# An expert-dispatch kernel: first input tile loaded in two pieces, and every third product computed on ScalarE

## The chip, the core and the metric

The kernel runs on one core of one Trainium2 chip. The core has several engines that run side by side, each with its own in-order stream of instructions: VectorE (DVE in the profile), ScalarE (ACT), GpSimd (POOL), SyncE (SP), and TensorE, which this kernel does not use. Data moves between the chip's main memory (HBM) and the on-chip memory (SBUF, 128 partitions) by 16 DMA engines. A DMA is issued by an instruction on one of the engines' streams and then runs on its own; another instruction that needs its data waits for its landing. The metric is device time in microseconds (us) of one execution, lower is better.

## The reference

The name speaks of dispatching tokens to experts, but the expert indices are not used in the result: each token's row is written twice, each time multiplied by one of that token's two weights.

```python
batch, seq, hidden, n_experts = 16, 1024, 512, 8
k = 2
"x":              (batch, seq, hidden) float32
"expert_weights": (batch, seq, k)      float32

x_expanded = x[:, :, np.newaxis, :].repeat(k, axis=2)
weights = expert_weights[..., np.newaxis]
return (x_expanded * weights).astype(np.float32)
```

There are 16,384 tokens of 512 float32 values. The input x is 33.5 MB and the output, with two scaled copies of every row, 67.1 MB. There is one multiplication for each output element.

## The kernel before

The 16,384 tokens are dealt to the 128 partitions, 128 consecutive tokens to each (`A_TOTAL` is 128). So a partition owns a contiguous stretch of x and a contiguous stretch of the output, and any group of tokens is a plain slice along the free dimension.

All weights are loaded once into `w_tile` (128 partitions x 256 numbers, 128 KB), by a DMA that SP issues (L45).

The loop on L47 runs over eight input tiles of `TX` = 16 tokens per partition. Each `x_tile` holds 128x8192 float32 numbers, 4 MB, and is loaded by one DMA that ScalarE issues (L49). ScalarE does nothing else in this kernel: its stream is eight load issues in order. `x_pool` has two buffers, so loads 0 and 1 are issued at the start, and load i+2 waits until the products of tile i are done.

Each input tile is worked off in two output tiles of `TO` = 8 tokens (L52). An `o_tile` is 128x8192 float32 as well, since every token has two rows: 4 MB again. It is filled by 16 VectorE instructions (L59), each of which multiplies one token's 512 numbers in every partition by one column of `w_tile`. Then SP issues the store of that output tile (L67). `o_pool` has four buffers, so the first product of output tile n+4 waits until the store of output tile n has landed. There are 16 stores and 256 products in all.

Two queues of DMA work come of this: the loads issued by ScalarE, and the weights and stores issued by SP. Both run on the same 16 DMA engines. The order of instructions on each engine is that of the program text, apart from small moves by the scheduler of the tile framework; the waits are put in by the framework, from the tiles' buffers.

Of the kernel before, what the change touches and what calls it, by code (L numbers as in the profile page):

```python
# [1 line left out]

# [4 lines left out]


@with_exitstack
def kernel(  # L10
    ctx: ExitStack,
    tc: tile.TileContext,
    x: bass.AP,
    expert_indices: bass.AP,
    expert_weights: bass.AP,
    out: bass.AP,
):
    nc = tc.nc

    batch, seq, hidden = x.shape  # L20
    k = expert_weights.shape[-1]
    P = nc.NUM_PARTITIONS
    ntok = batch * seq
    assert ntok % P == 0
    A_TOTAL = ntok // P

    xr = x.rearrange("b s h -> (b s) h").rearrange("(p a) h -> p (a h)", a=A_TOTAL)
    outr = out.rearrange("b s k h -> (b s) (k h)").rearrange(
        "(p a) n -> p (a n)", a=A_TOTAL
    )  # L30
    wr = expert_weights.rearrange("b s k -> (b s) k").rearrange(
        "(p a) k -> p (a k)", a=A_TOTAL
    )
    f32 = mybir.dt.float32
    row = k * hidden

    TX = 16
    TO = 8

    w_pool = ctx.enter_context(tc.tile_pool(name="w_pool", bufs=1))  # L40
    x_pool = ctx.enter_context(tc.tile_pool(name="x_pool", bufs=2))
    o_pool = ctx.enter_context(tc.tile_pool(name="o_pool", bufs=4))

    w_tile = w_pool.tile([P, A_TOTAL * k], f32)
    nc.sync.dma_start(out=w_tile, in_=wr)  # L45

    for i in range(A_TOTAL // TX):  # L47
        x_tile = x_pool.tile([P, TX * hidden], f32)
        nc.scalar.dma_start(  # L49
            out=x_tile, in_=xr[:, i * TX * hidden : (i + 1) * TX * hidden]  # L50
        )
        for j in range(TX // TO):  # L52
            o_tile = o_pool.tile([P, TO * row], f32)
            for t in range(TO):
                at = (j * TO + t) * hidden
                for kk in range(k):
                    c = (i * TX + j * TO + t) * k + kk
                    o = t * row + kk * hidden
                    nc.vector.tensor_scalar(  # L59
                        out=o_tile[:, o : o + hidden],  # L60
                        in0=x_tile[:, at : at + hidden],
                        scalar1=w_tile[:, c : c + 1],
                        scalar2=None,
                        op0=mybir.AluOpType.mult,
                    )
            first = (i * TX + j * TO) * row
            nc.sync.dma_start(out=outr[:, first : first + TO * row], in_=o_tile)  # L67


# [1 line left out]
_INS = ['x', 'expert_indices', 'expert_weights']  # L71
_OUTS = [((16, 1024, 2, 512), 'float32')]


# [23 lines left out]
```

## Time and profile before

| What | Value |
|---|---|
| Median of 6 runs | 242.32 us |
| Lowest and highest run | 241.01 and 243.82 us |
| The profiled execution's own time | 243.82 us |
| Span of the profiled execution, first to last instruction | 242.0 us |
| VectorE busy | 102.4 us, 42% of the span |
| Bytes moved by DMA | 100.81 MB |
| First load and weight load issued | 0.73 us |
| First product starts | 13.56 us |
| First store issued | 20.0 us |
| Last store issued | 209.1 us |

The profiled execution is the slowest of the six runs. Its span leaves out 1.8 us that lie around the first and the last instruction.

The page of the profile gives for each engine its busy time, then a strip of 40 equal slices of the span (about 6 us each), in which a digit is the busy share in tenths; for the DMA engines there is a strip of the same kind and a row of GB/s. A stretch is busy with DMA when its digit is 9. A row of the groups gives the line of the program, the engine, the operation, the tiles, the number of instructions, their busy time, the mean duration of one, and the idle time before them with what ended it. A view by windows gives the same for stretches that one picks: busy time of each engine with the number of instructions, the clock of TensorE, the busy share of the DMA engines, and the rate in GB/s. There, a DMA packet is counted whole, in the stretch where it ends, so that a short stretch can show a share above 1.

The eight loads were issued at 0.73, about 1.2, 26.35, 39.02, 65.40, 99.63, 128.56 and 158.85 us of the span.

### The profile page before, as it was taken

How to read it: one execution, taken by the hardware profiler on the slowest of the kernel's cores; microseconds unless marked ns; L12 is line 12 of the kernel's file. 1: busy time of each engine (PE TensorE's matmuls, PEld its weight loads, DVE VectorE, ACT ScalarE, POOL GpSimd, SP SyncE). 2: the span in 40 equal slices, each digit the busy share in tenths (PEclk: the TensorE clock that was granted, in tenths of full speed). 3: DMA queues.
4: the chain of work that ended last, by engine and by line, in shares of the span. 5: the costliest groups of instructions: out<-in, count | busy, mean ns of one | idle time of the engine just before them, and what ended most of it. 6: DMA issues, size and time to landing. Idle time of an engine off the chain costs nothing.

```text
span 242.0 us, 358 instructions
## 1 busy us (share of the span) xinstructions
DVE 102.4 (42%) x256; POOL 0.2 (0%) x4
## 2 busy tenths in 40 slices
DVE  0079994039803706490082820839008295500000
POOL 0000000000000000000000000000000000000000
DMA  7999999999999999999999999999999999999992
GB/s 276 439 433 422 433 348 428 433 433 417 433 433 428 433 433 433 433 428 433 395 433 433 433 433 433 435 428 433 433 422 433 433 433 433 433 433 433 433 433 97
DMA packets 3602, 100.81 MB, mean 417 GB/s; under 512 B 400, under 2 KB 528, under 8 KB 528
## 3 DMA queue, kind: packets, MB, share of 16 engines
q1 hardware_dynamic: 2448, 67.24, 64.6%
q10 hardware_dynamic: 1152, 33.55, 33.2%
q14 instruction: 2, 0.02, 0.0%
HBM read 33.69 MB, written 67.11 MB: 416 GB/s over the span
## 4 chain that ended last, share of the span: by engine, by line
DMA 52%; DVE 21%; another core or an unknown queue 13%; issue 0%; DVEq 0%
DMA out_dram<-o_tile 36%; DVE o_tile L59 21%; DMA x_tile<-in_x_dram 16%; DVEq L93 0%; DVEq L59 0%
## 5 line engine op out<-in xcount | busy, mean ns | idle before, releaser
L59 DVE TENSOR_SCALAR o_tile<-x_tile,w_tile 128x512 f32<-128x512 f32 x256 | 102.4, 480 | 106.6 <-DMA out_dram<-o_tile 75.4
L82 POOL MEMSET const-bfloat16-1.0<- 128x1 bf16 x1 | 0.1, 102 | 0.0
L82 POOL MEMSET const-uint8-127<- 128x1 uint8 x1 | 0.1, 102 | 0.0
L82 POOL MEMSET const-float32-1.0<- 128x1 f32 x1 | 0.1, 99 | 0.0
L82 POOL MEMSET const-float32-0.0<- 128x1 f32 x1 | 0.1, 98 | 0.2 <-issue 0.2
## 6 DMA issues: line engine op xcount, KB each, us to landing
out_dram<-o_tile SPq DMA_DIRECT2D x16, 4096.0 KB, 43.9
x_tile<-in_x_dram ACTq DMA_DIRECT2D x8, 4096.0 KB, 25.4
w_tile<-in_expert_weights_dram SPq DMA_DIRECT2D x1, 128.0 KB, 9.2
```

What stands on the lines that cost most here:

```text
L59: nc.vector.tensor_scalar(out=o_tile[:, o : o + hidden], in0=x_tile[:, at : at + hidden], scalar1=w_tile[:, c : c + 1], scalar2=None, op0= ...
L82: nc = _bacc.Bacc("TRN2", target_bir_lowering=False, num_devices=1)
```

## The change

The input tiles stand in a list of pieces; the first tile is loaded by two DMAs of 8 tokens (2 MB each), all others by one DMA of 16 tokens as before. Loads 0 and 1 are issued ahead of the loop, and load i+2 at the end of tile i's turn in the program text. Of the 256 products, those with a column number c that leaves 2 on division by 3 are computed by ScalarE (85 of them), the other 171 by VectorE. Buffers, tile sizes and stores stay: 16 stores of 4 MB, two input buffers, four output buffers.

```diff
+    AHEAD = 2
+    tiles = [[8, 8], [16], [16], [16], [16], [16], [16], [16]]
+    starts = [sum(map(sum, tiles[:i])) for i in range(len(tiles))]
...
-        nc.scalar.dma_start(
-            out=x_tile, in_=xr[:, i * TX * hidden : (i + 1) * TX * hidden]
-        )
+    def load(i):
...
+        x_tiles[i] = x_pool.tile([P, TX * hidden], f32, name="x_tile")
+        at = 0
+        for n in tiles[i]:
+            g = starts[i] + at
+            nc.scalar.dma_start(
+                out=x_tiles[i][:, at * hidden : (at + n) * hidden],
+                in_=xr[:, g * hidden : (g + n) * hidden],
+            )
+            at += n
...
+    def scale(out, in_, c):
+        w = w_tile[:, c : c + 1]
+        if c % 3 == 3 - 1:
+            nc.scalar.mul(out=out, in_=in_, mul=w)
+        else:
+            nc.vector.tensor_scalar(
...
+    for i in range(AHEAD):
+        load(i)
+    for i, pieces in enumerate(tiles):
+        x_tile = x_tiles.pop(i)
...
+        for t in range(sum(pieces)):
...
+                scale(
+                    o_tile[:, o : o + hidden],
+                    x_tile[:, t * hidden : (t + 1) * hidden],
+                    (starts[i] + t) * k + kk,
+                )
+            if t + 1 in ends or (t + 1) % TO == 0:
+                nc.sync.dma_start(
...
+        load(i + AHEAD)
```

In the built program, ScalarE's stream is as follows: the two pieces of load 0 and load 1; a load of the table for its activation function, which waits for the weights; 10 products of tile 0 and one of tile 1; load 2; 10 products of tile 1 and one of tile 2; load 3; 10 products of tile 2 and one of tile 3; load 4; 9 products of tile 3; load 5; 11 products of tile 4; load 6; 11 of tile 5; load 7; and the 21 products of tiles 6 and 7. So loads 2, 3 and 4 stand one product later than in the text, behind the first product of the next tile. VectorE takes 10 or 11 products for each output tile, ScalarE 5 or 6. SP's stream is as before, except that a store now waits for both engines.

More of the change, by code (lines that the diff above doesn't have):

```diff
@@ L38 @@
     TO = 8
+    AHEAD = 2
+    tiles = [[8, 8], [16], [16], [16], [16], [16], [16], [16]]
+    starts = [sum(map(sum, tiles[:i])) for i in range(len(tiles))]
+    assert sum(map(sum, tiles)) == A_TOTAL
     w_pool = ctx.enter_context(tc.tile_pool(name="w_pool", bufs=1))
-    x_pool = ctx.enter_context(tc.tile_pool(name="x_pool", bufs=2))
+    x_pool = ctx.enter_context(tc.tile_pool(name="x_pool", bufs=AHEAD))
     o_pool = ctx.enter_context(tc.tile_pool(name="o_pool", bufs=4))
@@ L45 @@
     nc.sync.dma_start(out=w_tile, in_=wr)
-    for i in range(A_TOTAL // TX):
-        x_tile = x_pool.tile([P, TX * hidden], f32)
-        nc.scalar.dma_start(
-            out=x_tile, in_=xr[:, i * TX * hidden : (i + 1) * TX * hidden]
-        )
[L52 to L67, printed above, removed]
+    x_tiles = {}
@@ new lines, in load @@
+    def load(i):
+        if i >= len(tiles):
+            return
+        x_tiles[i] = x_pool.tile([P, TX * hidden], f32, name="x_tile")
[13 more added lines that the diff above has]
+            nc.vector.tensor_scalar(
+                out=out,
+                in0=in_,
+                scalar1=w,
+                scalar2=None,
+                op0=mybir.AluOpType.mult,
+            )
@@ new lines @@
+    for i in range(AHEAD):
+        load(i)
+    for i, pieces in enumerate(tiles):
+        x_tile = x_tiles.pop(i)
+        ends = [sum(pieces[: j + 1]) for j in range(len(pieces))]
+        first = 0
+        for t in range(sum(pieces)):
+            if t % TO == 0:
+                o_tile = o_pool.tile([P, TO * row], f32)
+            for kk in range(k):
+                o = t % TO * row + kk * hidden
+                scale(
+                    o_tile[:, o : o + hidden],
+                    x_tile[:, t * hidden : (t + 1) * hidden],
+                    (starts[i] + t) * k + kk,
+                )
+            if t + 1 in ends or (t + 1) % TO == 0:
+                nc.sync.dma_start(
+                    out=outr[
+                        :, (starts[i] + first) * row : (starts[i] + t + 1) * row
+                    ],
+                    in_=o_tile[:, first % TO * row : (t % TO + 1) * row],
+                )
+                first = t + 1
+        load(i + AHEAD)
```

## The prediction

> **What bounds the kernel now.** I read the strip of DMA work first, because a kernel that only copies and scales can hardly be bound by anything else.
>
> ```profile
> span 242.0 us, 358 instructions
> DVE 102.4 (42%) x256; POOL 0.2 (0%) x4
> ...
> DMA  7999999999999999999999999999999999999992
> GB/s 276 439 433 422 433 348 428 433 433 417 433 433 428 433 433 433 433 428 433 395 433 433 433 433 433 435 428 433 433 422 433 433 433 433 433 433 433 433 433 97
> DMA packets 3602, 100.81 MB, mean 417 GB/s; under 512 B 400, under 2 KB 528, under 8 KB 528
> ```
>
> The DMA engines are full from the second slice to the last but one, nearly always at 433 GB/s; VectorE is busy for 42%. Next I cut windows by what is in flight: loads alone, the worst slice, loads beside stores, stores alone, the end.
>
> ```profile
> 5.00:21.00 16.00, 7.44 (x19) 0.00 (x0) 1.00 1.02 441
> ...
> 30.00:37.00 7.00, 7.00 (x19) 0.00 (x0) 1.00 1.01 348
> ...
> 132.00:150.00 18.00, 6.42 (x16) 0.00 (x0) 1.00 1.01 435
> ...
> 184.00:236.00 52.00, 17.44 (x44) 0.00 (x0) 1.00 1.00 434
> 236.00:238.00 2.00, 0.00 (x0) 0.00 (x0) 1.00 0.57 246
> 238.00:241.00 3.00, 0.00 (x0) 0.00 (x0) 1.00 0.08 33
> ```
>
> Loads alone go at 441 GB/s (434 to 441, as packets fall into windows), loads beside stores at 435, stores alone at 434. So the rate is the same whatever the mixture; one slice, 30 to 37 us, falls to 348 with the engines no less busy. Last, the waits and the chain:
>
> ```profile
> DVE o_tile L59 <- DMA out_dram<-o_tile: 75.4, 9, 12.9
> DVE o_tile L59 <- DMA x_tile<-in_x_dram: 27.2, 2, 13.6
> ...
> 13.56 12.77 DVE o_tile L59 x32
> 26.33 0.02 issue
> 26.35 26.14 DMA x_tile<-in_x_dram
> ```
>
> VectorE waits for stores to give buffers back, so it is the follower. Load 2, issued at 26.35, lands at 52.49 because it shares the engines. The chain names 32 products at 13.56 as a cause of load 2's issue, but while they ran, the strip shows the DMA engines full: that part of the chain costs nothing.
>
> The span as a sum: 100.81 MB at 434 GB/s are 232.3 us. The rest, 9.7 us, is: the first 5 us, which moved 1.23 MB (81 GB/s for 2 us, 357 for 3) where 434 GB/s would move 2.17, so 2.2 us lost; 30 to 37 us, (434-348) x 7 / 434 = 1.4 us; the last 6 us, which moved 0.59 MB of 2.60, so 4.6 us; and 1.5 us in small dips (116 to 120 us, at 401 GB/s, is 0.3 of it). Outside the span lie 243.82 - 242.0 = 1.8 us.
>
> **The change part by part.** No byte is added or removed except what ScalarE's table load may fetch.
>
> *The first tile in two pieces.* Load 0 lands at 13.54 us; its second half, 2.1 MB at 434 GB/s, is 4.8 us, so the first piece lands at about 8.7 us. The products also need the weights, which landed 9.2 us after their issue at 0.73, at 9.9. The first product thus starts between 8.7 and 9.9 instead of 13.56. This moves work ahead by 4 to 5 us on an engine that is no bound: until about 22 us the DMA engines have loads 0 and 1 to move (8.4 MB / 434 = 19.3 us from about 2.5). Saved on the path that sets the end: 0. The additional DMA is one more issue of 0.37 to 0.46 us on ScalarE, behind which only load 1 waits, and load 1 has 8 us until its turn. In the row, loads 0 and 1 were issued as two DMAs too, and 5 to 21 us shows no seam between them: cost 0. The Trainium skill, "DMA: Bandwidth & Descriptors", section "Anatomy of one DMA", gives for GpSimd-issued DMAs a time of 2.0 us plus bytes over 436 GB/s; if the additional DMA paid that fixed cost on the path, the sum would be 2.0 us more, an estimate against which the seamless 441 GB/s stands. "Perfetto Trace Analysis", section "DMA Optimizations", recommends splitting where the DMA engines are generally idle, and here the strip of nines says they are not.
>
> *A third of the products on ScalarE.* VectorE's 32 products took 12.77 us, 0.40 each, so an output tile took 6.4 us and will take 11 x 0.40 = 4.4 on VectorE. The trace has no ScalarE computation. The nearest row is VectorE's own mean, 0.48 for the same 128x512 product; I bound one ScalarE product by 0.40 (VectorE's pace) and 0.96 (twice its mean) and take 0.48. Six then take 2.4 to 5.8, 2.9 as taken, so an output tile is ready after 4.4 (at the worst 5.8) instead of 6.4. What hides this is the backlog of stores. In the phase with stores alone, one store needs 4.19 MB / 434 = 9.7 us, and three others are queued while one buffer is refilled; the refill would have to take longer than three stores, 29 us, to empty the queue. So ScalarE could cost 5 us a product before it decided. Cost and gain: 0. The Trainium skill, "ScalarE: Activation LUTs", section "What ACT_TABLE_LOAD costs", gives 1283 ns for the table load, and 186 ns plus 0.833 ns an element plus 93 for a pointer operand, 0.71 us here: inside the bounds, and the sum would be the same. The table load itself has no row; between 0 and the 6.4 us of a whole output tile it delays the first store only, under the cover of load 1; I take 0.
>
> *The first store earlier.* 8.7 or 9.9 plus 4.4 gives 13 to 14 us (16 if ScalarE is at its bounds) instead of 20.0. From about 15 us the store takes half the engines' time from load 1. What is left of load 1 then, 8.4 - (15 - 2.5) x 0.434 = 3.0 MB, goes at half the rate and lands near 29 us instead of 23. The total in flight is the same.
>
> *Load issues behind products.* Load 2 needs the products of tile 0 on both engines, done near 18 us, but it stands behind the first ScalarE product of tile 1, which needs load 1: it issues near 30 us instead of 26.35. Load 3 waits for load 2's landing, load 4 for load 3's, where before load 3 was issued at 39.02, 13 us before load 2 landed. An issued load needs some time before bytes flow: load 0 took 12.81 us for 9.7 us worth of bytes, so 3.1. So loads 2, 3 and 4 each begin 3 to 4 us after the one before has ended; loads pause more in this stretch than before. Queued on ScalarE behind the waiting product are the load and the rest of that tile's products, all of which need the same landing. The cover is the stores: at 29 us store 0's rest and store 1 (5 MB, 12 us) are queued, at 52 us stores 2 and 3 (8.4 MB, 19 us), at 74 us some three stores. Each exceeds 4 us by far. Price: 0, and 3 x 4 = 12 us if the cover were gone. Loads 5 to 7 wait for the same stores as before.
>
> *The rate while reads and writes mix.* Loads beside stores ran for some 117 us before (30 to 90, 104 to 123, 132 to 151, 163 to 182) and lost 1.4 + 0.3 + about 0.5 = 2.2 us there, 2%. Now 14 us of mixing are added (15 to 29 us). At the mean that is 0.3 us; the bounds are 0 (132 to 150 us lost nothing) and 20% of 14, 2.8 us (30 to 37 us). I take 0.1, since most mixed stretches lost nothing.
>
> Sum on the profiled execution: 243.82 + 0.1 = 243.9. That execution was the slowest of six; the median of the runs lies 1.5 us below it, about what its dip at 30 to 37 us cost. Against the median, 242.32 + 0.1, I predict 242.4 us.
>
> **Rivals.** *A, slower: mixing costs more.* One mechanism, the fall to 348 GB/s when a load starts against a store; its place is 15 to 29 us, where two pieces, load 1 and stores 0 and 1 now meet. At the rate of 30 to 37 us, 2.8 us: 245.1. It decides from 9% loss (1.2 us) on. For it: it is the largest dip and it came with a load's first bytes. Against: loads 6 and 7 started in the same way at full rate. 0.17.
>
> *B, slower: ScalarE's queue starves the DMA engines.* If the stores queued at 29, 52 and 74 us ran out, up to 12 us: 254. For it: loads 3 and 4 do lose their head start. Against: 12 to 19 us of stores at each place. 0.04.
>
> *C, faster: the losses shrink.* Stores spread earlier, so the dip at 30 to 37 us is gone (1.4 us) and the engines may end together: the last 6 us held 0.59 MB, 1.4 us at full rate, so even half of the 4.6 us tail is 2.3. With the dip alone 240.9, with both 238.6. For it: the tail is DMA engines that end apart. Against: nothing in the change touches the last 16 stores, of which four or five run alone at 434. 0.17.
>
> *D: the change doesn't keep the loads going.* Loads 2 to 4 then pause longer than before, at no price while stores are queued: 242.4 as well, and so part of the forecast. For it: the order of ScalarE's stream.
>
> **How the numbers follow.** Half a percent is 1.2 us, about what measuring this kernel tells from no change. Forecast, within that: 0.62, at 242.4. Slower: A and B, 0.21. Faster: C, 0.17. The range takes in the spread of the runs (241.0 to 243.8), C with the dip and half its other gain down to 240.0, and A nearly whole up to 244.9; B and C's extreme are left out.
>
> **What would show it.** First product near 9 us and first store issued at 13 to 16; ScalarE products of 0.4 to 0.96 us; loads 3 and 4 issued within 1 us of the landing before; a strip of nines with 434 GB/s through 29 to 34, 52 to 56 and 74 to 78 us; stores alone for the last 50 us. A digit below 9 in the middle of the strip makes the forecast wrong, by B; nines with GB/s below 420 through several slices, by A; a last slice well above 97 GB/s, with a shorter span, by C.

## The result, and the profile after

The changed kernel took 242.42 us (median of 35 runs, 241.57 to 244.0) beside 242.68 us for the kernel before (72 runs, 240.51 to 244.51). The ratio is 0.9995 with a 95% interval of 0.9981 to 1.0009. Nothing changed that can be measured, and the bound is tight: the interval excludes a gain or a loss of more than 0.2%.

The page of the changed kernel, the strips of busy time and the groups:

```profile
span 240.8 us, 377 instructions
DVE 68.9 (29%) x171; ACT 54.9 (23%) x86; POOL 0.2 (0%) x4
...
DVE  0680076007600760060070700607007155100000
ACT  0750073007300630060050500605005145000000
...
DMA  6999999999999999999999999999999999999993
GB/s 275 425 411 425 425 414 430 435 435 435 431 435 430 419 430 430 435 426 435 435 430 397 435 435 435 435 414 425 435 435 435 435 425 430 437 435 435 430 435 152
DMA packets 3747, 100.82 MB, mean 419 GB/s; under 512 B 416, under 2 KB 544, under 8 KB 544
...
L72 DVE TENSOR_SCALAR o_tile<-x_tile,w_tile 128x512 f32<-128x512 f32 x171 | 68.9, 481 | 136.9 <-DMA x_tile<-in_x_dram 69.0
L70 ACT ACTIVATE o_tile<-x_tile,w_tile 128x512 f32<-128x512 f32 x85 | 53.6, 709 | 143.5 <-DMA out_dram<-o_tile 74.6
L70 ACT ACT_TABLE_LOAD x1 | 1.3, 1283 | 6.0 <-DMA w_tile<-in_expert_weights_dram 6.0
```

VectorE lost a third of its work, 102.4 to 68.9 us, and ScalarE took it. The DMA strip is the same row of nines, and the bytes are the same but for 0.01 MB. The work that was made faster was waiting before, and now it waits longer: VectorE sat idle for 106.6 us ahead of its products before, and for 136.9 us now.

The start, from the timeline of the changed kernel (start, length, engine, instruction, count, and the idle time before with what ended it):

```profile
6.00 1.28 ACT L70 ACT_TABLE_LOAD   x1 [6.00 <-DMA w_tile<-in_expert_weights_dram]
8.36 3.17 ACT L70 ACTIVATE o_tile<-x_tile,w_tile 128x512 f32<-128x512 f32 x5 [1.07 <-DMA x_tile<-in_x_dram]
8.36 4.45 DVE L72 TENSOR_SCALAR o_tile<-x_tile,w_tile 128x512 f32<-128x512 f32 x11 [8.36 <-DMA x_tile<-in_x_dram]
12.90 27.47 SPq L97 DMA_DIRECT2D out_dram<-o_tile  x4
...
31.57 0.72 ACT L70 ACTIVATE o_tile<-x_tile,w_tile 128x512 f32<-128x512 f32 x1 [15.14 <-DMA x_tile<-in_x_dram]
...
31.63 0.33 ACTq L61 DMA_DIRECT2D x_tile<-in_x_dram  x1
...
55.55 0.72 ACT L70 ACTIVATE o_tile<-x_tile,w_tile 128x512 f32<-128x512 f32 x1 [17.13 <-DMA x_tile<-in_x_dram]
...
55.62 0.33 ACTq L61 DMA_DIRECT2D x_tile<-in_x_dram  x1
```

The first product starts 5.2 us earlier and the first store 7.1 us earlier. Load 2 is issued at 31.63 instead of 26.35 and load 3 at 55.62 instead of 39.02, each right behind the first ScalarE product of a tile that had just landed; load 4 follows in the same way at 79.54 instead of 65.40. So the loads pause longer than before: by the packets in the trace, no load moves from 30.0 to 36.1, from 53.9 to 59.4 and from 77.7 to 83.6 us. In the kernel before, loads paused from 23.3 to 30.6 us and then not until 90 us.

The stretch of the added mixing, and the three pauses, by windows (VectorE, ScalarE, GpSimd, clock, DMA share, GB/s):

```profile
14.00:29.00 15.00, 3.70 (x10) 2.43 (x4) 0.00 (x0) 1.00 0.99 404
...
30.00:36.00 6.00, 4.43 (x12) 4.43 (x8) 0.00 (x0) 1.00 1.02 431
54.00:60.00 6.00, 4.41 (x12) 4.46 (x8) 0.00 (x0) 1.00 1.01 426
78.00:84.00 6.00, 4.50 (x12) 3.84 (x7) 0.00 (x0) 1.00 0.98 410
```

Through the three pauses the DMA engines are full, with a share of 0.98 to 1.02 and 410 to 431 GB/s: stores fill them. Against 434 GB/s the three stretches together lose 0.5 us. From 14 to 29 us, where load 1 now shares with stores, 404 GB/s cost (434 - 404) x 15 / 434 = 1.0 us.

### The profile page after: what moved, and what is told of

Its sections match the earlier page's. It is cut to its first block, busy times and chain, and to the rows that moved or that the text cites. A ratio compares the mean times of both kernels' runs of the same rounds, so it can differ in the third digit from the quotient of the medians.

```text
span 240.8 us, 377 instructions
## 1 busy us (share of the span) xinstructions
DVE 68.9 (29%) x171; ACT 54.9 (23%) x86; POOL 0.2 (0%) x4
## 4 chain that ended last, share of the span: by engine, by line
DMA 71%; DVE 7%; another core or an unknown queue 6%; ACTq 0%; issue 0%; DVEq 0%; ACT 0%; SPq 0%
DMA out_dram<-o_tile 39%; DMA x_tile<-in_x_dram 32%; DVE o_tile L72 7%; ACTq L61 0%; DVEq L130 0%; DVEq L72 0%; ACT o_tile L70 0%; SPq L97 0%; ACTq L70 0%
## 5 line engine op out<-in xcount | busy, mean ns | idle before, releaser
L72 DVE TENSOR_SCALAR o_tile<-x_tile,w_tile 128x512 f32<-128x512 f32 x171 | 68.9, 481 | 136.9 <-DMA x_tile<-in_x_dram 69.0
L70 ACT ACTIVATE o_tile<-x_tile,w_tile 128x512 f32<-128x512 f32 x85 | 53.6, 709 | 143.5 <-DMA out_dram<-o_tile 74.6
L70 ACT ACT_TABLE_LOAD x1 | 1.3, 1283 | 6.0 <-DMA w_tile<-in_expert_weights_dram 6.0
```

Source lines behind the costliest of these rows:

```text
L70: nc.scalar.mul(out=out, in_=in_, mul=w)
L72: nc.vector.tensor_scalar(out=out, in0=in_, scalar1=w, scalar2=None, op0=mybir.AluOpType.mult,)
```

## The experiments

The theory to test: the bytes at about 434 GB/s set the time, and everything that the change moves lies under queued DMA work. The rivals: two effects that cancel; a fixed price for every DMA; pauses of the loads that cost something. Each comparison is with the kernel before, run on the same chip beside it. The ratios are given with their 95% intervals; they can differ from the quotient of the two medians by 0.1 or 0.2%. A difference in us is worked out from the ratio, unless it is said to be one of medians.

### The parts alone

Both are edits of the changed kernel. The first tile in two pieces, all products on VectorE:

```diff
-        if c % 3 == 3 - 1:
+        if False:
```

> The first tile in two pieces, all products on VectorE as before. Floor theory (bytes at 434 GB/s set the time, products and issue order lie under queued stores): first store issued near 15 us instead of 20, time 242.4 us, within 0.6. Rival, two parts that cancel: the earlier start is worth something and ScalarE's order gives it back; then this kernel alone is faster, 238 to 241 us.

Measured: 241.51 us beside 242.68, ratio 0.9959 (0.9932 to 0.9987).

A third of the products on ScalarE, the first tile in one piece:

```diff
-    tiles = [[8, 8], [16], [16], [16], [16], [16], [16], [16]]
+    tiles = [[16], [16], [16], [16], [16], [16], [16], [16]]
```

> A third of the products on ScalarE, in front of its load issues; first tile in one piece. Floor theory: 242.4 us, within 0.6, although loads 3 and 4 are issued only after the landing before. Rival, parts that cancel: with the split's gain missing, the pauses of the loads show, 244 to 247 us (3 pauses of 4 us, in part covered).

Measured: 242.80 us, ratio 1.0009 (0.9984 to 1.0035).

ScalarE's part is worth nothing, within 0.35%; its rival is dead, although loads 2 and 3 are issued at 26.75 and 50.57 us there, behind products as in the whole change. The split alone is 0.4% faster, about 1 us, which is more than the expected 0.6 and near the edge of its rival. Whether this is an effect of the split or of where the dips in the rate happened to fall is open; the interval starts at 0.1%, the whole change, which has the same split, does not show it, and no run separates the two. Cancelling gains of several microseconds are excluded: no part moves the time by more than 0.7%.

### Bytes, and the number of DMAs

The kernel before without its eighth load (the tokens of the last tile are computed from the seventh):

```diff
-        x_tile = x_pool.tile([P, TX * hidden], f32)
-        nc.scalar.dma_start(
...
+        if i < 7:
+            x_tile = x_pool.tile([P, TX * hidden], f32)
+        if i < 7:
+            nc.scalar.dma_start(
...
```

> The kernel before without its eighth load: the last 16 tokens of each partition are computed from tile 6. Floor theory: 4.19 MB less at 434 GB/s, 9.7 us less: 232.7 us. Rival (loads are hidden behind stores, and stores or products set the time): 240 to 242 us.

Measured: 232.57 us beside 242.89, ratio 0.9559 (0.9516 to 0.9602), which is 10.7 us less (9.7 to 11.8). The 9.7 us of the floor theory lie at the lower edge of the interval, and the rival is dead. This load of 4.19 MB, which lands more than 50 us before the end of the kernel, is worth its full time on the DMA engines. This is what it means that bytes set the time: a transfer that lands early still costs.

The changed kernel with all tiles in four pieces, which makes 64 loads and stores of 25:

```diff
-    tiles = [[8, 8], [16], [16], [16], [16], [16], [16], [16]]
+    tiles = [[4, 4, 4, 4] for _ in range(8)]
```

> The changed kernel with every tile loaded in four pieces of 1 MB, and so with stores of 2 MB: 64 loads and stores instead of 25. Floor theory: a DMA that is queued behind others costs nothing, 242.4 us, within 1. Rival, each DMA has a fixed cost on the path: 39 more DMAs at up to 3.1 us (what load 0 took beyond its bytes) is up to 120 us more, at a tenth of that still 12 us more.

Measured: 243.80 us beside 242.68, ratio 1.0045 (1.002 to 1.0069). This is 1.1 us above the kernel before and, by the medians, 1.4 us above the changed kernel's 242.42: 39 more DMAs cost 0.03 to 0.04 us each. Their rows are shorter too, so that this is a bound on the price of a DMA and not the price itself. Issued behind others, a DMA has next to no fixed price here; the one added by the change has none that could be seen.

### Mixing, and pauses of the loads

The kernel before with its loads on SP's queue:

```diff
-        nc.scalar.dma_start(
+        nc.sync.dma_start(
             out=x_tile, in_=xr[:, i * TX * hidden : (i + 1) * TX * hidden]
```

> The kernel before with its loads issued by SP as well, so that loads and stores follow one another in one queue and no longer mix. If the mixture of reads and writes causes the dips (about 2.2 us of the profiled execution before), 240 to 241.5 us. If the dips come anyway, 242.4, within 0.6. If a load that stands behind a store's wait leaves the DMA engines dry, 244 us or more and a digit below 9 within the strip.

Measured: 242.09 us beside 242.68, ratio 0.9988 (0.9961 to 1.0015), which is the "dips come anyway" of the expectation. The page still has dips:

```profile
GB/s 284 432 432 415 426 428 437 432 432 432 410 437 426 437 437 437 432 437 432 383 410 432 437 437 432 439 426 432 432 399 437 432 432 437 432 437 437 437 432 208
```

But the run did not take the mixing away. The one queue moves two loads, then four stores, and so on. At 434 GB/s from about 2 us on, two loads are 19 us and four stores 39, so that it should turn from stores to loads near 60, 118 and 177 us (an estimate). The slices at 410 (60 to 66 us), 383 and 410 (114 to 126) and 399 (174 to 180) lie there, and the one at 415 (18 to 24) at the first turn from loads to stores. The packets of the trace say the same: the 32 KB packets last 1.21 us in the median, and those of over 1.6 us lie in the first 4 us and within 6 us of a turn. So the dips of this kernel come where loads meet stores. Two queues pay for such a meeting in other places, and the time is the same; whether a kernel without any meeting would be faster was not run.

The changed kernel with three input and three output buffers:

```diff
-    AHEAD = 2
+    AHEAD = 3
-    o_pool = ctx.enter_context(tc.tile_pool(name="o_pool", bufs=4))
+    o_pool = ctx.enter_context(tc.tile_pool(name="o_pool", bufs=3))
```

> The changed kernel with three input and three output buffers instead of two and four, so that a load is nearly always queued. Floor theory: 242.4 us, within 0.7. Rival (pauses of the loads cost time): 239 to 241 us.

Measured: 242.42 us beside 242.89, ratio 0.9968 (0.9947 to 0.9989): 0.8 us less than the kernel before, with an interval that reaches from 0.3 to 1.3; the medians are 0.5 apart, and the changed kernel's own median is 242.42 as well. The rival's 239 to 241 us did not come. One more load in the queue, for one output buffer less, is worth at the most what a measurement can just see.

### The cover taken away

If the gains of the change are hidden under queued stores, they must come out when no store can be queued. Four kernels with one output buffer, with the edits of the parts as above:

```diff
-    o_pool = ctx.enter_context(tc.tile_pool(name="o_pool", bufs=4))
+    o_pool = ctx.enter_context(tc.tile_pool(name="o_pool", bufs=1))
```

The kernel before:

> The kernel before with one output buffer instead of four: no store is queued while products run, so the cover is gone. Each output tile then takes in turn 6.4 us of products, about 3 us until bytes flow and land, and 9.7 us of store: 19.2, sixteen times 307, and 13.6 at the head: 321 us, and more where a load shares the engines with a store (6 loads of up to 9.7 us: up to 379). A control for the three kernels beside it.

The changed kernel:

> The changed kernel with one output buffer. Floor theory: the change's gains are real and were hidden by queued stores; without them it shows 2 us less per output tile (4.4 instead of 6.4) and 5 us less at the head, 16 x 2 + 5 = 37 us less than the kernel before with one buffer. Rival, the load order costs as much as the products save: the pauses of the loads (4 us each, up to seven) take back 12 to 28 us of it.

Only the split:

> Only the first tile in two pieces, one output buffer. Floor theory: up to 5 us less than the kernel before with one buffer, as the first store starts earlier, or nothing if load 1 then shares with it. Rival (the split holds the whole gain): 20 us less or more.

Only ScalarE's products:

> Only the third of the products on ScalarE, one output buffer. Floor theory: 32 us less than the kernel before with one buffer (16 x 2.0). Rival (pauses of the loads cost once the cover is gone): 4 to 20 us less.

| One output buffer | Median us | Ratio to the kernel before (four buffers) |
|---|---|---|
| kernel before | 370.21 | 1.5253 (1.5146 to 1.536) |
| changed kernel | 340.75 | 1.4046 (1.3963 to 1.4129) |
| only the split | 370.75 | 1.5286 (1.5197 to 1.5374) |
| only ScalarE's products | 340.77 | 1.4049 (1.3967 to 1.4131) |

The pages of the kernel before and of the changed one, both with one buffer:

```profile
DMA  8994695364963649827398192991929909191927
...
L59 DVE TENSOR_SCALAR o_tile<-x_tile,w_tile 128x512 f32<-128x512 f32 x256 | 102.8, 481 | 255.5 <-DMA out_dram<-o_tile 173.2
```

```profile
DMA  7998499384991949929299193992939928294847
...
L72 DVE TENSOR_SCALAR o_tile<-x_tile,w_tile 128x512 f32<-128x512 f32 x171 | 69.2, 482 | 257.2 <-DMA out_dram<-o_tile 248.8
```

Now the DMA strip has gaps (ones to fours), and shorter products shorten the kernel: 29.5 us less by the medians with the whole change, 29.4 with ScalarE's part, nothing with the split. That is 1.8 us for each of 16 output tiles where 2.0 was expected. The earlier first store, for which I had expected up to 5 us, brings nothing: with the split alone it is issued at 14.84 us instead of 20.02, but it shares the engines with load 1, and the products that wait for it start at 33.79 instead of 33.47.

The rival of the load order is not tested by these four. With one output buffer the changed kernel issues load 2 right behind the last product of tile 0 (which ends at 34.04 + 4.44 = 38.48 us) and ahead of ScalarE's first product of tile 1, as the kernel before does:

```profile
34.04 4.44 DVE L72 TENSOR_SCALAR o_tile<-x_tile,w_tile 128x512 f32<-128x512 f32 x11 [21.24 <-DMA out_dram<-o_tile]
38.57 0.36 ACTq L61 DMA_DIRECT2D x_tile<-in_x_dram  x1
```

That first product comes at 61.12 us. So what the pauses of the loads would cost without queued stores stays open; with queued stores they cost nothing (act_only, and the windows above).

### The products doubled

Each product computed twice, in the kernel before and in the changed one (the same line around `scale`):

```diff
-                    nc.vector.tensor_scalar(
+                    for _ in range(2):
+                        nc.vector.tensor_scalar(
...
```

> The kernel before with each product computed twice: 12.8 us of VectorE per output tile instead of 6.4. By the threshold in the prediction (a refill may take as long as three queued stores, 29 us) nothing happens: 242.4 us. By a queue that must be filled first: the first store can be issued at 13.6 + 12.8 = 26.4 us while loads 0 and 1 end near 22, and the second one at 39.2 when the first is done at about 38, so the DMA engines run dry for some 6 and 3 us: 251 us.

Measured: 251.55 us beside 242.89, ratio 1.0347 (1.0304 to 1.039), which is 8.4 us more (7.4 to 9.5).

> The changed kernel with each product computed twice: 11 x 0.80 = 8.8 us per output tile, first store issued near 8.4 + 8.8 = 17 us, before the loads end. Both ways of counting: 242.4 us. If the kernel before with doubled products is at 251, the change is worth 9 us there, and nothing here.

Measured: 242.14 us beside 242.89, ratio 0.9976 (0.9947 to 1.0004).

Windows of the kernel before with doubled products:

```profile
22.00:28.00 6.00, 6.00 (x16) 0.00 (x0) 1.00 0.20 87
28.00:34.00 6.00, 6.00 (x16) 0.00 (x0) 1.00 1.02 437
34.00:40.00 6.00, 6.00 (x16) 0.00 (x0) 1.00 0.70 253
40.00:60.00 20.00, 20.00 (x52) 0.00 (x0) 1.00 0.94 395
```

And the stretch of 22 to 40 us in the changed kernel with doubled products:

```profile
22.00:28.00 6.00, 5.83 (x16) 1.82 (x3) 0.00 (x0) 1.00 0.84 355
28.00:34.00 6.00, 6.00 (x16) 6.00 (x11) 0.00 (x0) 1.00 1.09 433
34.00:40.00 6.00, 6.00 (x16) 5.88 (x10) 0.00 (x0) 1.00 1.03 437
```

In the first, loads 0 and 1 have ended and no store is there yet: the rate falls to 87 GB/s, (434 - 87) x 6 / 434 = 4.8 us lost, then to 253, 2.5 us, and to 395 over 20 us, 1.8 us. Together this is 9.1 us, where the kernel before loses 1.6 in the same 38 us (416 GB/s): 7.5 us of the 8.4 are lost here, at the start. The changed kernel issues its first store at 17.75 us, before the loads end, and loses 1.1 us in the first of its windows and nothing in the others. So the change does do something: it moves the point at which products would decide. With single products neither kernel is at that point. Which of the two parts moves it was not run.

## Why the prediction was right, and where its steps were not

**The bound.** Right, and shown by taking bytes out (9.7 us foretold, 10.7 measured, 9.7 to 11.8). The forecast was 242.4, the result 242.42. That they agree to 0.02 us is luck: the forecast added 0.1 to 242.32, the median of six runs, and with 72 runs that median is 242.68. What holds is the ratio.

**The first tile in two pieces.** Right that it moves the start of the products (8.36 us; 8.7 to 9.9 foretold) and costs nothing as an additional DMA: 0.03 to 0.04 us each in the kernel with 39 more. The weights, which might hold the first product back until 9.9 us, landed 5.2 us after their issue instead of 9.2 and held nothing back. The fixed 2.0 us that the Trainium skill's "DMA: Bandwidth & Descriptors", section "Anatomy of one DMA", gives for DMAs issued by GpSimd does not appear on the path here, where ScalarE and SP issue DMAs into a full queue. The step that gave a price of 0 to the earlier start may be off by up to 1 us (the split alone, 0.4% faster), which stays open.

**ScalarE's products.** I took 0.48 us between bounds of 0.40 and 0.96. One lasts 709 ns, and six in a row take 3.79 us, 0.63 each. The estimate of 0.71 us from the Trainium skill's figures ("ScalarE: Activation LUTs", section "What ACT_TABLE_LOAD costs") agrees with this, and its 1283 ns for the table load is the row's 1283 too. The value taken was too low, the conclusion holds: VectorE's 4.45 us are still the longer part.

**The threshold was wrong.** The prediction said that a refill would have to take longer than three queued stores, 29 us, or 5 us a product, before it decided. At best that holds for a single late refill when the queue is full, which no run tried. At 12.8 us per output tile, the kernel before already takes 8.4 us longer, because the queue has to be filled at the start, while the loads run out at about 22 us. And if every refill is late, products decide once they take longer than the DMA engines need per output tile on average, 232.3 / 16 = 14.5 us, whatever the queue's depth (an estimate from the sum; not run). My cover was counted in depth where it should have been counted in the state at the start, and in rate.

**Load issues behind products.** Right in mechanism: load 2 at 31.63 (30 foretold), loads 3 and 4 within 0.2 us of the landing before, the DMA engines full through all three pauses. The pauses were put at 3 to 4 us and lasted 5.5 to 6.1.

**The added mixing.** The sum had 0.1 us, bounds 0 to 2.8. The changed kernel's 14 to 29 us lost 1.0 us in its profiled execution, and the same stretch of the kernel before 0.5 (419 GB/s), so 0.5 more; and the dip of 1.4 us at 30 to 37 us did not come back. So the place of rival A was right, and its size a third at the most. What the prediction did not see is that other kernels with two queues show such a dip as well, once, early, where loads and stores first meet: 348 GB/s from 30 to 37 us without load 7, as in the kernel before; 355 GB/s from 18 to 24 us with ScalarE's part alone; 360 there with the split alone; 385 from 14 to 22 us in the changed kernel. The window of the kernel without load 7:

```profile
30.00:37.00 7.00, 7.00 (x18) 0.00 (x0) 1.00 1.01 348
```

That reads as a dip that the change moved and not one that it added, and it fits the mechanism of rival A; with one profile of each kernel it is not shown. It also contradicts a reading of the prediction, that this dip made the profiled execution 1.5 us slower than the median: the profiled execution without load 7 has the same dip and took 232.63 us, beside a median of 232.57. What made the profiled execution of the kernel before slow stays open.

**The tail.** As foretold, stores alone at 433 GB/s, and DMA engines that end apart:

```profile
184.00:234.00 50.00, 10.91 (x28) 8.01 (x13) 0.00 (x0) 1.00 1.00 433
...
236.00:238.00 2.00, 0.00 (x0) 0.00 (x0) 0.00 (x0) 1.00 0.38 164
238.00:241.00 3.00, 0.00 (x0) 0.00 (x0) 0.00 (x0) 1.00 0.05 22
```

The sign that the prediction named for rival C did come: a last slice of 152 GB/s instead of 97, and a span of 240.8 us instead of 242.0. It does not speak for C, since the execution profiled before was the slowest of its six, and the one-queue kernel, which leaves the last stores as they are, shows 208 there.

No version that does the whole work beats both kernels by more than a measurement just shows. The lowest is the split alone, 241.51 us.

## What to carry to other kernels

Where the DMA strip is full at one rate from end to end, count the bytes, and ask of a change only whether it removes any or leaves the engines dry somewhere; faster products show when the cover is taken away (29 us here), and not before, and an earlier first store showed nothing even then, because it shared the engines with a load. Work out the cover as a rate for what comes every time, and as a depth only for what comes once (this is argued above, not run), and look at the start, where the queue is not full yet. An issue that is put behind a compute instruction on the same engine does delay transfers (load 3 by 16.6 us here), which cost nothing here while the other queue had work; without that work it was not tried.

## What the runs showed of the hardware

The weights, 128 KB in rows of 1 KB on SP's queue, landed 8.0 to 10.4 us after their issue where ScalarE's queue had loads of 32 KB per partition (six profiles), 5.2 to 6.6 us beside pieces of 16 KB (six), and 4.2 us beside pieces of 8 KB (one). The rows of the issues in the kernel before, the changed kernel and the one with four pieces:

```profile
w_tile<-in_expert_weights_dram SPq DMA_DIRECT2D x1, 128.0 KB, 9.2
```

```profile
w_tile<-in_expert_weights_dram SPq DMA_DIRECT2D x1, 128.0 KB, 5.2
```

```profile
w_tile<-in_expert_weights_dram SPq DMA_DIRECT2D x1, 128.0 KB, 4.2
```

This fits two queues that take turns packet by packet, so that a small transfer waits for the long packets of the other queue; it was not tested by itself. In the kernel with one queue the weights stand ahead of the loads on the same queue, and they landed after 2.2 us; the first product started at 13.66 us there, beside 13.56 in the kernel before. A small operand that is needed first would do well to be issued ahead of large ones on their queue. Where it landed later, it cost nothing in these kernels: load 0 or its first piece landed later still.
